# A hybrid attention, state-space and expert-retrieval block on one core: three groups of token tiles instead of four, and a reordered start

## The chip, the cores and the metric

The kernel runs on one core of one Trainium2 chip. The metric is the device time of one execution in microseconds (us). The engines are called TensorE (PE; PEld its weight loads), VectorE (DVE), ScalarE (ACT), GpSimd (POOL) and SyncE (SP). SP issues most transfers, POOL the gathers.

## What is computed

One block over 1024 latent tokens and 256 context tokens, 1024 wide, all in float32:

```python
z_lat = modulate(h_lat, sh_a, sc_a) @ w_in      # query, kv, rope key, state-space input, two gates
z_ctx = modulate(h_ctx, csh_a, csc_a) @ w_in
att_lat = block_attention(q_l, concat([k_c, k_l]), concat([v_c, v_l]))   # 8 heads, 1280 keys
s5_lat, s5_ctx = s5_mixer(su_l, su_c, ...)      # both directions, complex diagonal, 32 groups
out_lat = branch_merge(att_lat, s5_lat, gm_l, gs_l, w_glu, w_out)
h_lat = layer_norm(ALPHA * h_lat + g_a * out_lat, ln1_g, ln1_b)
f_lat = peer(modulate(h_lat, sh_f, sc_f), wq, keys, u_tab, v_tab)
h_lat = layer_norm(ALPHA * h_lat + g_f * f_lat, ln2_g, ln2_b)
```

`peer` finds for each token and each of 8 heads the 16 best of 16384 experts by product keys, 128 experts a token, takes the dot product of the token with each expert's row of `u_tab`, and sums the experts' rows of `v_tab` with the gelu of these products as weights.

## The kernel before, in words

The latent tokens lie in eight tiles of 128, the context in two. The program is one function, `block_kernel`. Each engine works its instructions off in a fixed order, which the compiler's scheduler makes from the order of the code, from priorities (`tc.high_priority(PRIO[gi])`, one offset a group) and from `tc.issue_after(...)`, which lets what stands under it come only behind a given instruction.

**The start (L118 to L330).** Large weights go through `wload` (L214), 1 MB tiles of a pool `w` with four buffers. `load_x` (L246) loads two token tiles with one such transfer, so they take weight buffers too. Eight 1 MB tiles of the modulation weights `w_mod_a` (L278) are multiplied with the condition into the bank `pmr` (L282). Four ACT copies (L292) bring its four rows to `mrow`, four transposes (L295) make `pm`, and VectorE turns it into the column `modc` (L297, L300). For each of ten tiles, `project` (L302) then normalises (L175), transposes, writes the modulated tile `hm` (L318, L320), stores it to `hm_d`, and multiplies it with the state-space part of the input weights (`pc`, L327), whose result goes to `us_d`. Beside this, `modulation_rows` (L349) works through 16 further 1 MB weights.

**The state space (L364 to L660).** VectorE and POOL build tables of powers (L367 to L491). The input is reloaded as `U` by eight transfers of 16 x 32 x 192 (L651). `compress` (L660) reloads `hm` tile by tile (L664) and makes compressed keys and values; the state products (L582, L583) need `U` and the tables.

**Groups (L1404).** `front` takes a group of token tiles through attention (scores L858 to L862, their maxima L863, probabilities L805, weighted values L809), the gates (products L239 to L241), and `close` (output product L954), and hands back a generator, `route`: the expert query (`pqr` L1066, `pz` L1074) and the two top-16 searches (L994 to L998). That generator is stepped `TSTEP` times at each step of the next group's attention. Each group loads all keys, values, gate and output weights, and splits keys and weights anew into two parts (L233 on ACT, L234 on VectorE). `PREP` says how early the next group's query projection (`prepare`, `pa` L770) begins.

**Retrieval.** For tiles 0 and 1, POOL gathers for each of 128 expert numbers one row per token from `peer_u` (L1271, tile `ub`), VectorE multiplies and sums (L1275, a "score"), and then POOL gathers rows of `peer_v` token by token (L1351), which TensorE sums (`acc` L1356, a "weighted row"). `HOLDS` keeps scores behind marks in the routes. Tiles 2 to 5 take another way: their weights are spread into a table (`spread`, L1147 to L1156), and `dense` goes over all experts (`turn` L1235 to L1237, `fd` L1196 to L1198) with the retrieval of tiles 6 and 7 on VectorE beside it.

The order is set by tables at the head of the file:

```python
GROUPS = ((0,), (1, 2), (3, 4, 5), (6, 7))
TSTEP = (2, 2, 2)
SUBS = (((0,),), ((0, 1),), ((0, 1, 2),), ((0, 1),))
PRIO = (0, 1500, 1500, 3000, 2000)
HOLDS = {0: [(M0, S0)] + [("r1.%d" % h, S0 + P0 * (h + 1)) for h in range(8)], ...}
```

Of the kernel before, what the change touches and what calls it, by code (L numbers as in the profile page):

```python
# [8 lines left out]
F32 = mybir.dt.float32  # L9
# [21 lines left out]
WBUFS = 4  # L31
# [3 lines left out]
SCB = (3, 3, 2, 2)  # L35
SC2 = (1, 1, 1, 1)
CAB = (1, 1, 1, 1)
OHB = (1, 1, 1, 1)
QHB = (2, 2, 1, 1)
H2B = 1  # L40
HMB = 2
GROUPS = ((0,), (1, 2), (3, 4, 5), (6, 7))
DENSE = (2, 3, 4, 5)
VEC = (6, 7)
TSTEP = (2, 2, 2)
TPRE = (0, 0, 0)
# [27 lines left out]
S0 = 36
P0 = 128
S1 = 100
P1 = 128
M0 = "p2"
M1 = "p3"
# [3 lines left out]
KENG = ((), (), (), ())  # L83
GENG = ((), (), (), ())
# [5 lines left out]
def block_kernel(ctx: ExitStack, tc: tile.TileContext, a: dict, out: bass.AP):  # L90
# [163 lines left out]
    SY.dma_start(bcol, a["b_col"])  # L254
# [13 lines left out]

    load_x(0)
# [5 lines left out]
    GP.memset(mrow, 0.0)  # L275
    pmr = bank("mm", "pmr")
    for k in range(8):
        wt = wload(a["w_mod_a"][k], [128, 2048])  # L278
        if k == XLOAD:
            load_x(1)  # L280
        for j in range(4):
            PE.matmul(pmr[32 * j:32 * j + 2, :], sil[:, k, :], wt[:, j * 512:(j + 1) * 512],  # L282
                      start=(k == 0), stop=(k == 7), tile_position=(0, 32 * j))
    with tc.issue_after(last[0].ins if hasattr(last[0], 'ins') else last[0]):
        w1 = s5.tile([128, 8, 512], F32, tag="U", name="w1")
        for k in range(0, 8, 2):
            SY.dma_start(w1[:, k:k + 2, :], a["w_in1"][:, k:k + 2, 384:896])
# [12 lines left out]
    V.tensor_scalar(modc[:, 1], modc[:, 1], 1.0, None, op0=ADD)  # L300

    def project(n):  # L302
        lat = n - 2
        ctxt = lat < 0
        cond = 1 if ctxt else 0
        if n % 2 == 0:
            if n > 2:
                load_x(n // 2)
            normalize(xt[n:n + 2])
# [12 lines left out]
        transpose8(x, put, "S")  # L322
        S.dma_start(hm_d[n], hm.rearrange("p a b -> p (a b)"))
# [43 lines left out]
    V.tensor_scalar(cni, cni, -1.0, None, op0=MUL)  # L367
# [123 lines left out]
    V.tensor_tensor(dsk, dsk, eye[0:16, 0:16].unsqueeze(1).to_broadcast([16, 32, 16]), op=MUL)  # L491

# [154 lines left out]
    wk = [wload(a["w_ukv"][:, k, :], [128, 2048]) for k in range(2)]  # L647
    U = s5.tile([128, 32, 192], F32, tag="U", name="U")
# [114 lines left out]
    def prepare(gi, P, w, hms):  # L763

        cqT = R["q"][1]
        for i, hmT in enumerate(hms):
# [4 lines left out]
            nq = (P or W).tile([128, 384 if P else 2048], F32, tag="nq" if P else "w", bufs=2 if P else WBUFS, name="nq")[:, 0:384]  # L771
# [9 lines left out]
        if P:  # L781
            P.release()
# [812 lines left out]
```

## Time and profile before

| | |
|---|---|
| runs | 3733.66, 3748.12, 3753.72 us, median 3748.12 |
| profiled execution | 3734.93 us, span of the trace 3733.2 us |
| instructions | 54383 |
| mean granted TensorE clock | 0.948 |
| busy share | TensorE 90%, VectorE 79%, GpSimd 40%, ScalarE 35% |
| moved | 1032.46 MB, 277 GB/s over the span |
| of it gathers | 536.94 MB in 1024 gathers |

The stages follow one another on TensorE: start and projections to about 180 us, state space, keys and values to 473, group (0) to 645, group (1, 2) to 981, attention of (3, 4, 5) to 1341, its gates to 1520 and close to 1628, attention of (6, 7) to 1924, its gates to 2064, the spread to 2212, and the dense part to the end. A stage's rows say more than the shares of the whole run.

### The profile page before, as it was taken

Reading aid. Unit: us, or ns where it says so; the run is one execution under the profiler, and the core shown is the slowest. Engines: PE = TensorE matmul, PEld = TensorE weight load, DVE = VectorE, ACT = ScalarE, POOL = GpSimd, SP = SyncE. Lnnn points to the kernel's source line nnn. Section 1 sums busy time; section 2 is a strip of 40 time slices with the busy share of each in tenths; the row PEclk is TensorE's granted clock in tenths of the full one; section 3 lists DMA queues with packets and bytes.
Section 4 is the critical chain, followed back from the end, with each engine's and each line's share of the span. In section 5 each row is a group of like instructions: output and inputs, shape, how many; then the busy total and the mean of one; then the engine's idle time right before and its main releaser. Section 6 shows DMA issues by size and latency. Waiting matters only on the chain.

```text
span 3733.2 us, 54383 instructions
## 1 busy us (share of the span) xinstructions
PE 3359.1 (90%) x20022; PEld 2733.2 (73%) x20022; DVE 2956.9 (79%) x6996; ACT 1297.7 (35%) x2329; POOL 1491.9 (40%) x1254
## 2 busy tenths in 40 slices
PE   5978888979779989869999969999999999999997
PEld 3745577869667668757769758878888888888885
DVE  7358755685798879689968877888888888889895
ACT  2223353443123444033345443333333333333332
POOL 5045400041355564443442100265655555546540
PEclk7978999989889989979999979999999999999998
DMA  8742276476698898987898763599999999989992
GB/s 280 236 85 73 89 264 228 156 301 244 224 347 309 316 338 324 362 308 289 295 355 314 296 232 124 181 368 340 330 342 333 339 335 340 340 325 355 340 328 79
DMA packets 348714, 1032.46 MB, mean 277 GB/s; under 512 B 46592, under 2 KB 142080, under 8 KB 322592
## 3 DMA queue, kind: packets, MB, share of 16 engines
q0 software_dynamic: 147456, 536.94, 39.3%
q1 hardware_dynamic: 164032, 462.20, 34.9%
q10 hardware_dynamic: 36960, 29.86, 2.5%
q8 instruction: 157, 2.57, 0.3%
q14 instruction: 109, 0.89, 0.1%
HBM read 961.27 MB, written 67.62 MB: 276 GB/s over the span
## 4 chain that ended last, share of the span: by engine, by line
PE 56%; DVE 9%; issue 8%; DMA 7%; ACT 2%; POOL 2%; DVEq 0%; POOLq 0%; ACTq 0%
PE turn L1235 6%; PE turn L1237 6%; PE turn L1236 6%; PE fd L1196 5%; PE fd L1197 5%; PE fd L1198 5%; DMA vb<-in_peer_v,eiT 4%; DVE ub L1275 3%; PE po L954 2%; PE acc L1356 2%; PE pqr L1066 2%; PE pe L1153 2%; DMA ub<-in_peer_u,ei 2%; POOL ub L1271 1%; PE po L809 1%
## 5 line engine op out<-in xcount | busy, mean ns | idle before, releaser
L1271 POOL DMA_INDIRECT ub<-in_peer_u,ei x512 | 654.9, 1279 | 1212.9 <-DVE ub L1275 438.4
L1275 DVE SCALAR_TENSOR_TENSOR ub<-ub,h 128x1024 f32<-128x1024 f32 x512 | 616.3, 1217 | 59.5 <-DMA ub<-in_peer_u,ei 59.2
L1318 POOL DMA_INDIRECT vb<-in_peer_v,ei x256 | 361.8, 1413 | 268.2 <-DVE f L1321 205.5
L1351 POOL DMA_INDIRECT vb<-in_peer_v,eiT x256 | 288.7, 1128 | 400.4 <-PE acc L1356 324.8
L1235 PE MATMUL turn<-hh,u 128*128 128x512 f32 x1024 | 401.7, 392 | 0.0
L1236 PE MATMUL turn<-hh,u 128*128 128x512 f32 x1024 | 400.2, 391 | 0.0
L1237 PE MATMUL turn<-hl,u 128*128 128x512 f32 x1024 | 400.1, 391 | 0.0
L1197 PE MATMUL fd<-v,kpe_l 128*128 128x512 f32 x887 | 351.7, 397 | 1.5 <-DVE kpe_l L234 1.5
L1198 PE MATMUL fd<-v,kpe_h 128*128 128x512 f32 x887 | 349.6, 394 | 0.0
L1196 PE MATMUL fd<-v,kpe_h 128*128 128x512 f32 x887 | 339.3, 396 | 0.0
L1321 DVE SCALAR_TENSOR_TENSOR f<-vb,zz,f 128x1024 f32<-128x1024 f32 x254 | 325.4, 1281 | 2.8 <-DMA vb<-in_peer_v,ei 0.2
L1239 ACT ACTIVATE act<-turn 128x512 f32<-128x512 f32 x128 | 76.6, 598 | 578.7 <-PE turn L1237 578.6
L233 ACT CAST v<-w 128x1024 fp32r<-128x1024 f32 x128 | 134.7, 1053 | 269.1 <-PE fd L1197 269.0
L1235 PEld LDWEIGHTS turn<-hh,u 128*128 128x128 f32 x1024 | 192.3, 188 | 42.0
L1237 PEld LDWEIGHTS turn<-hl,u 128*128 128x128 f32 x1024 | 192.3, 188 | 41.9
L1236 PEld LDWEIGHTS turn<-hh,u 128*128 128x128 f32 x1024 | 192.3, 188 | 40.4
L1356 PE MATMUL acc<-vb,diag 128*32 128x256 f32 x2048 | 159.8, 397 | 51.1 <-DMA vb<-in_peer_v,eiT 51.0
L1198 PEld LDWEIGHTS fd<-v,kpe_h 128*128 128x128 f32 x887 | 166.8, 188 | 41.4
L1196 PEld LDWEIGHTS fd<-v,kpe_h 128*128 128x128 f32 x887 | 166.9, 188 | 40.8
L1197 PEld LDWEIGHTS fd<-v,kpe_l 128*128 128x128 f32 x887 | 166.9, 188 | 40.5 <-DVE kpe_l L234 1.8
L234 DVE TENSOR_TENSOR v<-w,v 128x1024 fp32r<-128x1024 f32 x128 | 156.2, 1221 | 33.4 <-ACT v L233 32.8
L1241 DVE TENSOR_TENSOR act<-act,gt 128x512 f32<-128x512 f32 x128 | 88.6, 692 | 118.2 <-ACT act L1239 117.9
(421 smaller groups left out, 8143.2 us busy)
## 6 DMA issues: line engine op xcount, KB each, us to landing
w<-in_peer_uT SPq DMA_DIRECT2D x64, 1024.0 KB
w<-in_peer_v SPq DMA_DIRECT2D x64, 1024.0 KB
w<-in_peer_wq SPq DMA_DIRECT2D x32, 1024.0 KB
gT_d<-stage SPq DMA_DIRECT2D x16, 2048.0 KB
gt<-gT_d SPq DMA_DIRECT2D x32, 1024.0 KB
vh<-v_d SPq DMA_DIRECT2D x32, 640.0 KB
w<-k_d SPq DMA_DIRECT2D x32, 640.0 KB
w<-in_w_mod_b SPq DMA_DIRECT2D x16, 1024.0 KB
```

The lines of the kernel that those rows point to most:

```text
L1196: PE.matmul(o, ah[:, ts], vh[:, cs], start=first, stop=False)
L1197: PE.matmul(o, al[:, ts], vh[:, cs], start=False, stop=False)
L1198: return PE.matmul(o, ah[:, ts], vl[:, cs], start=False, stop=final)
L1235: PE.matmul(turn, uh[:, k, :], hh[:, k, :], start=(k == 0), stop=False)
L1236: PE.matmul(turn, ul[:, k, :], hh[:, k, :], start=False, stop=False)
L1237: PE.matmul(turn, uh[:, k, :], hl[:, k, :], start=False, stop=(k == 7))
L1271: GP.indirect_dma_start(out=ub, out_offset=None, in_=a["peer_u"], in_offset=bass.IndirectOffsetOnAxis(ap=ei[:, s:s + 1], axis=0))
L1275: V.scalar_tensor_tensor(ub, ub, 1.0, h2, op0=MUL, op1=MUL, accum_out=dots[:, s:s + 1])
L1318: GP.indirect_dma_start(out=vb, out_offset=None, in_=a["peer_v"], in_offset=bass.IndirectOffsetOnAxis(ap=ei[:, s:s + 1], axis=0))
L1321: V.scalar_tensor_tensor(f, vb, z[:, s:s + 1], f, op0=MUL, op1=ADD)
L1351: GP.indirect_dma_start(out=vb, out_offset=None, in_=a["peer_v"], in_offset=bass.IndirectOffsetOnAxis(ap=eiT[:, t:t + 1], axis=0))
L1356: PE.matmul(acc[d // 2][o:o + 32, 256 * (d % 2):256 * (d % 2) + 256], dg[:, q, jj, :], vb[:, d * 256:(d + 1) * 256], start=False, stop=Fal ...
```

## The change

The tiles are now taken in three groups, (0, 1, 2), (3, 4, 5) and (6, 7); the route of the first group runs in two parts, tile 0 and then tiles 1 and 2. The holds on the scores of tiles 0 and 1 are gone, the steps of the route per attention step are 3 and 2. At the start, token tiles are loaded into buffers that are still empty (`ckvT` and a widened `U`) with two 512 KB transfers a pair, the second pair and several small tables behind the last modulation weight, and the row `mrow` comes over in two copies of 128 x 256, one on ACT and one on VectorE. The second half of the state-space tables is issued only after `modc`. The first two reloads of `hm` stand ahead of `U`, further ones two tiles ahead of their use, and `U` comes in 32 pieces.

```diff
-GROUPS = ((0,), (1, 2), (3, 4, 5), (6, 7))
+GROUPS = ((0, 1, 2), (3, 4, 5), (6, 7))
-TSTEP = (2, 2, 2)
+TSTEP = (3, 2)
-SPLIT = (False, False, True, False)
-SUBS = (((0,),), ((0, 1),), ((0, 1, 2),), ((0, 1),))
+SPLIT = (False, True, False)
+SUBS = (((0,), (1, 2)), ((0, 1, 2),), ((0, 1),))
-PREP = (0, 9, 9, None)
+PREP = (9, 9, None)
-PRIO = (0, 1500, 1500, 3000, 2000)
+PRIO = (0, 1500, 3000, 2000)
-RAT = 3
+RAT = 2
-HOLDS = {0: [(M0, S0)] + [("r1.%d" % h, S0 + P0 * (h + 1)) for h in range(8)],
-         1: [(M1, S1)] + [("r2.%d" % h, S1 + P1 * (h + 1)) for h in range(8)],
-         6: [("t3", 0)]}
+HOLDS = {6: [("t2", 0)]}
...
-        x = wload((a["x"][2 * i - 2:2 * i] if i else a["ctx"]).rearrange("l p d -> p l d"), [128, 2, D])
-        xt.extend([x[:, 0, :], x[:, 1, :]])
+        pair = [w1x[:, 8 + 2 * j:10 + 2 * j].rearrange("p a b -> p (a b)") if i % 2 else ckvT[:, j] for j in range(2)]
+        for j, t in enumerate(pair):
+            SY.dma_start(t[:, 0:D], a["x"][2 * i - 2 + j] if i else a["ctx"][j])
+            xt.append(t[:, 0:D])
...
-    for j in range(4):
-        S.copy(mrow[32 * j:32 * j + 2, :], pmr[32 * j:32 * j + 2, :])
+    S.copy(mrow[:, 0:256], pmr[:, 0:256])
+    V.tensor_copy(mrow[:, 256:512], pmr[:, 256:512])
...
-    V.tensor_scalar(modc[:, 1], modc[:, 1], 1.0, None, op0=ADD)
+    held = V.tensor_scalar(modc[:, 1], modc[:, 1], 1.0, None, op0=ADD)
...
+    hold = tc.issue_after(held.ins)
+    hold.__enter__()
+    V.tensor_scalar(cni, cni, -1.0, None, op0=MUL)
...
+    hold.__exit__(None, None, None)
...
+    load_hm(0)
+    load_hm(1)
     U = s5.tile([128, 32, 192], F32, tag="U", name="U")
-    ul = us_d.rearrange("b (g c) l j -> l c (b g) j", c=16)
-    for l in range(8):
-        SY.dma_start(U[16 * l:16 * l + 16], ul[l])
+    for b in range(4):
+        ul = us_d[b].rearrange("(g c) l j -> l c g j", c=16)
+        for l in range(8):
+            SY.dma_start(U[16 * l:16 * l + 16, 8 * b:8 * b + 8], ul[l])
```

How the orders change, at three places. First SyncE's transfers at the end of the projections, before:

```order
L357 DMA mod_d<-rows 1x512 x4
L214 DMA w<-in_w_ukv 128x2048
L664 DMA hm<-hm_d 128x1024
L651 DMA U<-us_d 16x32x192 x7
L664 DMA hm<-hm_d 128x1024
L651 DMA U<-us_d 16x32x192
L664 DMA hm<-hm_d 128x1024 x4
```

and now:

```order
L354 DMA mod_d<-rows 1x512 x4
L652 DMA hm<-hm_d 128x1024 x2
L660 DMA U<-us_d 16x8x192 x32
L533 DMA T<-kd_d_74 128x8x64
L652 DMA hm<-hm_d 128x1024 x3
```

The second `hm` has moved from behind seven pieces of `U` to ahead of all; the third stands behind all 32.

Second, VectorE around the column `modc` (lines 404 to 490 before are tables), before:

```order
L409 TENSOR_TENSOR pwi<-sq_1243,sq_1244 128x32
L297 TENSOR_TENSOR modc<-pm,bcol 128x32
L462 TENSOR_TENSOR sq_1243<-aim 128x32
L489 COPY ri<-pwi 64x256
L490 COPY ri<-pwi 64x256
L300 TENSOR_SCALAR modc<-modc 128x16
L463 TENSOR_TENSOR kf<-kf,sq_1243 128x32
L320 TENSOR_SCALAR hm<-tp,modc 128x128 x3
```

and now:

```order
L429 COPY uli<-u8i 128x32
L287 COPY mrow<-pmr 128x256
L292 TENSOR_TENSOR modc<-pm,bcol 128x32
L295 TENSOR_SCALAR modc<-modc 128x16
L452 MEMSET pwr 128x32
L453 MEMSET pwi 128x32
L454 TENSOR_TENSOR pwr<-mag,ucs 128x32
L315 TENSOR_SCALAR hm<-tp,modc 128x128 x3
```

`modc` was VectorE's instruction 222 and is now its 151st; the powers `pwr`, `pwi` and all behind them have moved past it.

Third, VectorE at the first score (the instruction that reads `ub`; `mx` are attention's maxima, `ef` and `ei` the end of a route), before, where it stands after 55 of 192 maxima:

```order
L799 TENSOR_REDUCE smx_6414<-sm3_6329 128x1
L863 TENSOR_REDUCE mx_6384<-pS_6385 128x1
L800 RECIPROCAL smx_6414<-smx_6414 128x1
L1275 SCALAR_TENSOR_TENSOR ub_17881,dots_17878<-ub_17881,h2_17879 128x1024
L863 TENSOR_REDUCE mx_6384<-pS_6392 128x1
L863 TENSOR_REDUCE mx_6384<-pS_6399 128x1
```

and now, after 108 of 192:

```order
L1045 SCALAR_TENSOR_TENSOR ef_7341<-pi_8301 128x64
L1114 CAST ei_8538<-ef_7341 128x128
L1120 CAST eiT_8542<-ptE_8540 128x128
L1286 SCALAR_TENSOR_TENSOR ub_17492,dots_17489<-ub_17492,h2_17490 128x1024
L1005 MAX V16_8553<-sc_8578 128x8 x2
L1286 SCALAR_TENSOR_TENSOR ub_17495,dots_17489<-ub_17495,h2_17490 128x1024
```

The first score has moved from the attention of tiles 1 and 2 into the middle of that of tiles 3 to 5, between the route of tile 0 and those of tiles 1 and 2. Counted over VectorE's whole order, 167 scores stood ahead of the 145th maximum (the end of that attention) and 131 do now, all of them behind the 108th.

## Rows read from the trace of the kernel before

**Rows 1.** Busy time by stretch of the run; x is the count of instructions.

```profile
core 0: us, PE busy (x) PEld busy (x) DVE busy (x) ACT busy (x) POOL busy (x), PEclk, DMA share, GB/s
60.00:210.00 150.00, 120.91 (x939) 96.85 (x938) 55.26 (x146) 31.39 (x67) 28.32 (x37) 0.89 0.82 229
180.00:218.00 38.00, 15.54 (x46) 9.12 (x46) 2.35 (x13) 3.12 (x10) 0.00 (x0) 0.69 1.00 124
480.00:560.00 80.00, 67.21 (x429) 60.20 (x429) 46.79 (x123) 48.55 (x123) 0.00 (x0) 0.89 0.78 287
560.00:660.00 100.00, 83.14 (x568) 75.59 (x567) 56.91 (x121) 35.30 (x60) 0.00 (x0) 0.97 0.62 226
660.00:850.00 190.00, 161.31 (x1091) 145.24 (x1089) 146.70 (x495) 86.18 (x229) 52.83 (x40) 0.94 0.64 230
850.00:980.00 130.00, 117.45 (x838) 111.93 (x838) 74.03 (x173) 30.52 (x43) 1.87 (x2) 0.95 0.57 203
981.00:1341.00 360.00, 304.99 (x2178) 244.00 (x2176) 317.93 (x1045) 125.39 (x326) 204.91 (x183) 0.93 0.89 323
1341.00:1520.00 179.00, 156.99 (x1292) 142.58 (x1292) 147.59 (x308) 70.76 (x79) 89.39 (x65) 0.93 0.91 342
1520.00:1628.00 108.00, 77.62 (x458) 58.44 (x458) 85.83 (x229) 8.89 (x17) 53.12 (x44) 0.83 0.87 322
1628.00:1924.00 296.00, 281.44 (x2189) 214.26 (x2190) 239.55 (x1073) 116.30 (x281) 130.18 (x127) 0.98 0.85 307
2064.00:2212.00 148.00, 106.73 (x776) 88.21 (x766) 123.17 (x362) 66.54 (x81) 18.33 (x18) 0.86 0.71 264
```

**Rows 2.** Groups of TensorE, 20 to 60 us: busy, mean ns, idle before and releaser.

```profile
L295 PE MATMUL pm<-eye,mrow 128*128 128x128 f32 x4 | 1.1, 428 | 6.9 <-ACT mrow L292 6.9
L327 PE MATMUL pc<-hm,w 128*128 128x128 f32 x26 | 5.3, 384 | 6.6 <-DVE hm L320 6.6
```

**Rows 3.** Timeline, 38 to 60 us: start, length, engine, line, operation, idle before.

```profile
38.06 1.89 PE L282 MATMUL pmr<-w,sil 128*2 128x512 f32 x8 [1.86 <-DMA w<-in_w_mod_a]
41.73 2.37 ACT L175 ACTIVATE w<-w,off,rs_y 128x1024 f32<-128x1024 f32 x2 [19.26 <-DMA w<-in_w_in]
44.39 2.34 ACT L292 COPY mrow<-pmr 2x512 f32<-2x512 f32 x4
```

**Rows 4.** TensorE's group after the projections, then tile U: ns min/median/max, first and last start.

```profile
L668 PE MATMUL pb<-w,hm 128*128 128x320 f32 (+1 forms) x56 | 19.6, 508 | 18.5 <-DMA hm<-hm_d 18.5
L651 SPq DMA_DIRECT2D U<-us_d x8: 334/654/3927, 180.5 to 193.6; - x8
L582 PE MATMUL pS<-U,Pm x32: 299/299/351, 217.9 to 232.6; 128*64 128x160 f32 x32
```

**Rows 5.** Timeline: the first product of tile 0's query projection.

```profile
472.87 2.36 PE L770 MATMUL pa<-w 128*128 128x128 f32 x19 [0.72 <-ACT zt L639]
```

**Rows 6.** Groups of TensorE and VectorE, 981 to 1341 us.

```profile
L1066 PE MATMUL pqr<-h2T,w 128*128 128x128 f32 x512 | 62.7, 277 | 1.9 <-ACT att L810 1.4 <-ACT qh L1070 0.5
L1074 PE MATMUL pz<-keysT,qh 128*128 128x128 f32 x64 | 10.5, 286 | 2.0 <-ACT sc L1075 1.4 <-ACT att L810 0.5
L1356 PE MATMUL acc<-vb,diag 128*32 128x256 f32 x416 | 30.6, 387 | 5.1 <-DMA vb<-in_peer_v,eiT 5.0
L1275 DVE SCALAR_TENSOR_TENSOR ub<-ub,h 128x1024 f32<-128x1024 f32 x133 | 160.7, 1216 | 16.2 <-DMA ub<-in_peer_u,ei 16.1
L863 DVE TENSOR_REDUCE mx<-pS 128x1 f32<-128x512 f32 (+1 forms) x72 | 41.7, 593 | 5.7 <-PE pS L862 5.7
```

**Rows 7.** All score gathers by their line, and the page's row of their queue.

```profile
L1271 POOL DMA_INDIRECT ub<-in_peer_u,ei x512: 932/1144/2957, 766.6 to 3224.7; - x171
q0 software_dynamic: 147456, 536.94, 39.3%
```

**Rows 8.** Transfers: the gather queue 473 to 980 us, then all from 980 to 2212 us.

```profile
q0 software_dynamic: 6048, 22.02, 11.8%
...
DMA packets 97118, 389.44 MB, mean 316 GB/s; under 512 B 10304, under 2 KB 16704, under 8 KB 88896
```

More of the change, by code (lines that the diff above doesn't have):

```diff
@@ L34 @@
 RB = 6
[L35 to L39, printed above, removed]
+SCB = (2, 2, 2)
+SC2 = (1, 1, 1)
+CAB = (1, 1, 1)
+OHB = (1, 1, 1)
+QHB = (1, 1, 1)
 H2B = 1
 HMB = 2
-GROUPS = ((0,), (1, 2), (3, 4, 5), (6, 7))
+GROUPS = ((0, 1, 2), (3, 4, 5), (6, 7))
 DENSE = (2, 3, 4, 5)
 VEC = (6, 7)
-TSTEP = (2, 2, 2)
-TPRE = (0, 0, 0)
+TSTEP = (3, 2)
+TPRE = (0, 0)
 CHUNK = 32
@@ L50 @@
 VCUT = 2
-STB = (1, 1, 1, 1)
-SPLIT = (False, False, True, False)
-SUBS = (((0,),), ((0, 1),), ((0, 1, 2),), ((0, 1),))
+STB = (1, 1, 1)
+SPLIT = (False, True, False)
+SUBS = (((0,), (1, 2)), ((0, 1, 2),), ((0, 1),))
 CENG = "VVVV"
@@ L61 @@
 XLOAD = 4
-GSIDE = ('right', 'right', 'right', None)
-CSIDE = ("right", "right", "right", None)
+GSIDE = ('right', 'right', None)
+CSIDE = ("right", "right", None)
 SETTLE = 2
-PREP = (0, 9, 9, None)
-GSPLIT = (True, True, True, True)
+PREP = (9, 9, None)
+GSPLIT = (True, True, True)
 GWB = 2
-EBS = (2, 2, 2, 4)
+EBS = (2, 2, 4)
 EBANK = "S"
-PRIO = (0, 1500, 1500, 3000, 2000)
+PRIO = (0, 1500, 3000, 2000)
 PACE = 8
-RAT = 3
+RAT = 2
 TWAIT = 2
[L74 to L79, printed above, removed]
-HOLDS = {0: [(M0, S0)] + [("r1.%d" % h, S0 + P0 * (h + 1)) for h in range(8)],
-         1: [(M1, S1)] + [("r2.%d" % h, S1 + P1 * (h + 1)) for h in range(8)],
-         6: [("t3", 0)]}
-KENG = ((), (), (), ())
-GENG = ((), (), (), ())
+HOLDS = {6: [("t2", 0)]}
+KENG = ((), (), ())
+GENG = ((), (), ())
 EVERY = (1, 2, 1)
@@ L253, in block_kernel @@
     bcol = pre.tile([128, 16], F32, tag="bcol", name="bcol")
-    SY.dma_start(bcol, a["b_col"])
     S.activation(sil, ccT, func=AF.Tanh, scale=0.5)
@@ L267, in block_kernel @@
     dsk = s5.tile([16, 32, 16], F32, tag="dsk", name="dsk")
+    w1x = s5.tile([128, 12, 512], F32, tag="U", name="w1")
     load_x(0)
@@ L284, in block_kernel @@
     with tc.issue_after(last[0].ins if hasattr(last[0], 'ins') else last[0]):
-        w1 = s5.tile([128, 8, 512], F32, tag="U", name="w1")
+        w1 = w1x[:, 0:8]
+        SY.dma_start(bcol, a["b_col"])
         for k in range(0, 8, 2):
-            SY.dma_start(w1[:, k:k + 2, :], a["w_in1"][:, k:k + 2, 384:896])
+            loaded = SY.dma_start(w1[:, k:k + 2, :], a["w_in1"][:, k:k + 2, 384:896])
+    with tc.issue_after(loaded.ins):
+        load_x(1)
+        SY.dma_start(iota, a["iota"])
+        V.tensor_copy(ranks, iota[:, 0:16].unsqueeze(2).to_broadcast([128, 16, 16]))
         for t, nm in ((bre, "s5_b_re"), (bim, "s5_b_im"), (cre, "s5_c_re"), (cni, "s5_c_im")):
@@ L305, in project @@
         cond = 1 if ctxt else 0
[L306 to L309, printed above, removed]
+        if n == 0:
+            normalize(xt[0:2])
+        if n % 2 and n + 2 < NT:
+            normalize(xt[n + 1:n + 3])
         x = xt[n]
@@ L322, in project @@
         transpose8(x, put, "S")
+        if n % 2 and n // 2 + 2 < NT // 2:
+            load_x(n // 2 + 2)
         S.dma_start(hm_d[n], hm.rearrange("p a b -> p (a b)"))
@@ L647, in block_kernel, with load_hm @@
     wk = [wload(a["w_ukv"][:, k, :], [128, 2048]) for k in range(2)]
+    hms = []
+    def load_hm(n):
+        hms.append(pre.tile([128, 8, 128], F32, tag="hm", bufs=HMB, name="hm"))
+        SY.dma_start(hms[n].rearrange("p a b -> p (a b)"), hm_d[n])
+    load_hm(0)
+    load_hm(1)
     U = s5.tile([128, 32, 192], F32, tag="U", name="U")
-    ul = us_d.rearrange("b (g c) l j -> l c (b g) j", c=16)
-    for l in range(8):
-        SY.dma_start(U[16 * l:16 * l + 16], ul[l])
-    SY.dma_start(qng, a["q_norm_g"])
+    for b in range(4):
+        ul = us_d[b].rearrange("(g c) l j -> l c g j", c=16)
+        for l in range(8):
+            SY.dma_start(U[16 * l:16 * l + 16, 8 * b:8 * b + 8], ul[l])
     kng = pre.tile([128, 2], F32, tag="kng", name="kng")
-    SY.dma_start(kng, a["kv_norm_g"])
     ropt = pre.tile([128, 8, 128], F32, tag="ropt", name="ropt")
-    SY.dma_start(ropt, a["rope_tok"])
+    with tc.issue_after(loaded.ins):
+        SY.dma_start(qng, a["q_norm_g"])
+        SY.dma_start(kng, a["kv_norm_g"])
+        SY.dma_start(ropt, a["rope_tok"])
     def compress(n):
@@ L662, in compress @@
         ctxt = lat < 0
-        hm = pre.tile([128, 8, 128], F32, tag="hm", bufs=HMB, name="hm")
-        SY.dma_start(hm.rearrange("p a b -> p (a b)"), hm_d[n])
+        hm = hms[n]
         pb = bank("mm", "pb")
@@ L668, in compress @@
             PE.matmul(pb[:, 0:w], hm[:, k, :], w1b[k // 4][:, k % 4, 0:w], start=(k == 0), stop=(k == 7))
+        if n + 2 < NT:
+            load_hm(n + 2)
         junk = pre.tile([128, 256], F32, tag="junk", name="junk")
@@ L748, in prepare_loads @@
         grp = GROUPS[gi]
-        P = pool("P%d" % gi) if gi else None
+        P = pool("P%d" % gi)
         SY.dma_start(R["q"][2], a["rope_feat"][:, :, 128 * grp[0]:128 * grp[0] + 128 * len(grp)])
@@ L753, in prepare_loads @@
             w = [w[:, 0], w[:, 1], wload(a["w_cq"][2], [128, 8, 128])]
-            return P, w, [wload(hm_d[grp[0] + 2].rearrange("p (a b) -> p a b", a=8), [128, 8, 128])]
+            two = wload(hm_d[2:4].rearrange("l p (a b) -> p l a b", a=8), [128, 2, 8, 128])
+            return P, w, [two[:, 0], two[:, 1], wload(hm_d[4].rearrange("p (a b) -> p a b", a=8), [128, 8, 128])]
         w = P.tile([128, 3, 8, 128], F32, tag="wcq", name="wcq")
@@ L770, in prepare @@
                     PE.matmul(pa[:, j * 128:(j + 1) * 128], hmT[:, k, :], w[j][:, k, :], start=(k == 0), stop=(k == 7))
-            nq = (P or W).tile([128, 384 if P else 2048], F32, tag="nq" if P else "w", bufs=2 if P else WBUFS, name="nq")[:, 0:384]
+            nq = P.tile([128, 384], F32, tag="nq", bufs=2, name="nq")
             ss = cols.tile([128, 1], F32, tag="ss", name="ss")
@@ L780, in prepare @@
                 S.activation(cqT[:, j, i * 128:(i + 1) * 128], pt[:, j, :], func=AF.Copy, scale=qng[:, j:j + 1])
-        if P:
-            P.release()
+        P.release()
     def open_queries(gi):
```

7 lines of the change are left out of this document (1 added, 6 removed).

## The prediction

> **What bounds the kernel now.** I read the busy time of each engine in stretches first, since one average over 3733 us hides different limits. From 180 to 218 us almost nothing runs: TensorE 15.5 of 38 us, VectorE 2.4, while the transfer engines are 1.00 busy for only 124 GB/s. From 480 to 980 us, attention, gates and output projection of tile 0 and then of tiles 1 and 2, no engine is full: TensorE is busy 67.2 of 80, 83.1 of 100, 161.3 of 190 and 117.5 of 130 us, and the transfer share is 0.57 to 0.78. From 981 to 1341 us, attention of tiles 3 to 5 with the routes of tiles 1 and 2 and the score gathers of tiles 0 and 1 beside it, VectorE (317.9 of 360) and the transfers (0.89, 323 GB/s) are both near full; after that TensorE or the transfers are [rows 1]. The dense part after 2212 us keeps its instructions, and its inputs come from a finished table, so I cost the change there at nothing.
>
> The second view is who ended each idle time. At the start TensorE waits 6.9 us for ACT's copy of the modulation row and 6.6 us for VectorE's first `hm` [rows 2]; ACT had been held 19.3 us by a load that its normalisation needed, and its four copies take 2.3 us [rows 3]. Behind the projections TensorE waits 18.5 us for the reload of `hm`, the second of which SP issues behind seven of the eight `U` transfers [rows 4].
>
> **The change part by part.** The sum is made against the profiled execution, 3734.9 us (span 3733.2); the median of the runs shown is 3748.1, 13 us above it. A difference of about 0.5%, 19 us, is what a measurement of this kernel can tell from no change.
>
> *Start.* The second token pair now stands behind most modulation weights, so the last weight may land a little sooner, which I leave out. ACT is no longer in the middle of its normalisation when the row is ready: the last product ends at 39.95 and the first copy starts at 44.39, 4.4 us, and the copies take 2.3 [rows 3]. Two half copies, one on each of two engines, cost some 0.5 us (an estimate from 0.58 us for one of the four). That gives 4.4 + 1.8. VectorE reaches `modc` and `hm` without the second half of the tables in front of them: 6.6 us [rows 2]. Together −13. Bounds: −15, and 0 if the stream of modulation weights behind it sets the pace to 210 us (share 0.82, 229 GB/s); TensorE's 120.9 of 150 us speaks for most of it staying [rows 1]. The held table work moves to where VectorE is busy 55.3 of 150 us [rows 1]: nothing, unless the state space comes to wait for it.
>
> *Into the state space.* Two `hm` reloads now stand ahead of `U`, and the first state product needs one quarter of `U`. Before, it starts at 217.9 us [rows 4]. Now TensorE has two tiles of compression and the products (0.3 us each) to do while `U` lands. But `hm` of the third tile is issued behind all 32 pieces, and one issue of `U` takes SP 0.65 us at the median [rows 4]: 21 us, so to about 202 with the projections' end at 181. I take −20 of the 22 us that TensorE idles there. Bounds: −24, and 0, since the transfer engines are full at 124 GB/s [rows 1] and may end `U` no sooner. If each piece costs its issue, 24 more pieces are 16 us, and the term becomes −4. The Trainium skill, "DMA: Bandwidth & Descriptors", section "Rules for kernel authors", speaks against this edit too: it asks for transfers of at least a MiB and calls those under 64 KB mostly overhead, and here pieces of 384 KB become 96 KB; no row shows `U` in such pieces, and by that rule the sum would lean to the −12 that a term of −4 gives.
>
> *Three tiles in one group.* The two groups ahead of tiles 3 to 5 take 508 us, from 473 [rows 5] to 981. TensorE is busy 429 us from 480 to 980 [rows 1]; the route of tile 0 moves out, half of the 73.2 us that two routes take later [rows 6], and 392 us stay. Keys, values, gate and output weights are loaded and split once instead of twice, which is off TensorE. Its busy share was 0.84 in attention with one tile, 0.90 in the gates of two, 0.95 beside routes (281.4 of 296) [rows 1]; three tiles in turn, without a route, I put at 0.94: 415 us, so −93. Bounds 0.98 and 0.86: 400 and 456, −108 and −52.
>
> *What is pushed into the next group.* Attention of tiles 3 to 5 now carries three routes instead of two. Its first half has tile 0's route and no score, as the order shows. TensorE's work of that half is (305.0 − 30.6 for `acc` − 73.2 for the two routes) / 2 + 36.6 for one route = 137 us [rows 1, 6], at 0.94 some 147. In the second half fall as many scores as this stage had before (131): 160.7 us of VectorE. Its other 157 us of 317.9 were attention and two routes; the maxima are 41.7 of it [rows 6], and I put attention at 75 (an estimate), half of it now past: 160.7 + 82 + 37 = 280, on an engine nearly full 290. The stage: 147 + 290 = 437 against 360, so +77. Bounds: 260 to 330 for the second half, +47 to +117.
>
> *Later stages.* In the new order 10 more scores fall beside the close of group 1, 27 more beside the attention of tiles 6 and 7, and some 20 more weighted rows into the last stretch. Ten times 1.216 us [rows 6] on a VectorE busy 85.8 of 108 [rows 1]: +10. Twenty-seven, 33 us, on one busy 239.6 of 296, where TensorE ends the stage [rows 1]: +9, bounds 0 and +35. A weighted row is eight products, 30.6 / 52 = 0.6 us of TensorE [rows 6], 20 are 12 us in a stretch with 106.7 of 148 busy [rows 1]: +2, bounds −5 and +12.
>
> Sum: −13 − 20 − 93 + 77 + 10 + 9 + 2 = −28. On the profiled execution that is 3707, on the median 3720; I say **3715**.
>
> **The rivals.**
> *Nothing is gained* (chance 0.22). Retrieval starts when the first tile's route is ready: at 767 us now [rows 7], about 473 − 33 + 415 + 147 = 1002 then. From 980 to 2212 us 389 MB moved, 316 GB/s; 42 gathers (22 MB) came earlier [rows 8]. In the new order these come later too, and half an attention's keys and values (5 MB) earlier: 406 MB stand behind the first gather. My forecast asks for 406 MB in 1182 us, 343 GB/s; at 336 dense begins at 2212 as before, and the head start of 235 us is given back: 3730 to 3760. For it: transfers 0.85 to 0.89 busy in every stage between. Against it: 1341 to 1520 ran at 342 with TensorE at 157.0 of 179 [rows 1], so transfers alone did not set the pace.
>
> *Slower* (0.18). The same queue, one step on: with the gathers packed closer, the transfers stay at the 323 of the stage from 981 to 1341 us, and 406 MB take 1257 us. Dense begins at 2259, +47: 3782 to 3795. It decides from about 330 GB/s down, as a mean from the first gather to the dense part.
>
> *Much more* (0.14). VectorE fills its gaps (42 us idle of 360 [rows 1]), the second half takes 260, the later stages absorb the extra rows, and three tiles run at 0.98: −13 − 20 − 108 + 47 + 10 = −84, or 3651 to 3664.
>
> *The start does not hold* (0.06). `U` in 32 pieces or the held tables delay the state space, the first two terms fall to −4 together, and the sum to +1: 3736 to 3749.
>
> **How the numbers follow.** The forecast (3690 to 3735) keeps 0.40. "Much more" and the bounds of the terms give the low end 3655; half of "slower" the high end 3782. Faster by over 19 us holds "much more" and nearly all of the forecast: 0.53. Slower by as much holds "slower" and the upper edge of "nothing": 0.19. Same: 0.28.
>
> **What would show it.** Right: the first product of the input projection at about 42 us instead of 54.6, the first state product before 190, attention of tiles 3 to 5 starting near 855 instead of 983 and lasting about 437; the first gather near 1002, and 340 GB/s from there to the dense part. Wrong: if nothing is gained by 473 us, one of the two first terms fell; if the stage of tiles 3 to 5 lasts over 480 us with VectorE waiting for `ub`, the transfers set it; if VectorE is busy there without a wait and the stage is as long, I undercounted its route work.

## The result: 0.7% slower, and the profile after

The changed kernel takes 3767.3 us (median of 7 runs, 3755.8 to 3784.5), the kernel before, in runs beside it, 3741.1 us: a ratio of 1.0069 (95% interval 1.0044 to 1.0094), 26 us slower where 33 us faster than the first median was forecast. The profiled execution has a span of 3754.0 us, 20.8 us above that of before.

This is the changed kernel by stretch, cut at its own stages; it answers to [rows 1]:

```profile
core 0: us, PE busy (x) PEld busy (x) DVE busy (x) ACT busy (x) POOL busy (x), PEclk, DMA share, GB/s
34.00:166.00 132.00, 113.08 (x892) 96.14 (x892) 80.86 (x224) 34.28 (x66) 39.28 (x52) 0.88 0.74 264
166.00:205.00 39.00, 36.87 (x231) 26.11 (x230) 22.37 (x52) 11.41 (x37) 6.72 (x11) 0.87 0.85 155
486.00:683.00 197.00, 176.87 (x1128) 151.63 (x1127) 87.03 (x222) 111.53 (x282) 0.00 (x0) 0.98 0.26 89
683.00:794.00 111.00, 108.22 (x900) 107.81 (x901) 43.37 (x64) 32.78 (x43) 0.00 (x0) 1.00 0.45 162
868.00:1015.00 147.00, 135.30 (x904) 116.89 (x905) 90.49 (x384) 61.31 (x177) 0.99 (x1) 0.97 0.36 123
1015.00:1147.00 132.00, 105.03 (x709) 92.02 (x707) 120.43 (x421) 35.86 (x95) 72.34 (x67) 0.91 0.89 321
1147.00:1240.00 93.00, 32.24 (x128) 25.73 (x127) 91.78 (x253) 4.17 (x12) 71.42 (x56) 0.61 0.93 334
1240.00:1335.00 95.00, 73.54 (x591) 49.58 (x591) 70.17 (x263) 27.75 (x74) 55.44 (x54) 0.89 0.86 314
1335.00:1494.00 159.00, 146.79 (x1211) 132.96 (x1210) 142.04 (x295) 69.61 (x76) 81.78 (x57) 0.95 0.93 356
1605.00:1936.00 331.00, 296.21 (x2161) 219.74 (x2157) 279.35 (x1144) 119.96 (x285) 174.58 (x158) 0.92 0.89 320
```

Read it from the top. The hole of 38 us behind the projections is gone (36.9 of 39 us busy). Attention and gates of three tiles run with TensorE busy 177 of 197 and 108 of 111 us, and from the first query projection at 452 up to 1015 us POOL does nothing and the transfers are busy for less than half of the time (0.26 to 0.45 in these rows). Then the opposite: from 1015 to 1240 us VectorE is busy 212 of 225 us, the transfers 0.89 and 0.93, POOL issues gathers again, and between 1147 and 1240 us TensorE works 32 of 93 us. Who held it is in TensorE's timeline of that stretch (start, length, operation, idle before and its releaser):

```profile
1143.15 3.74 PE L1077 MATMUL pqr<-h2T,w 128*128 128x128 f32 x32
1146.72 0.38 PE L816 MATMUL pt<-eye,P 128*128 128x128 f32 x2
1172.48 1.22 PE L1085 MATMUL pz<-keysT,qh 128*128 128x128 f32 x4 [25.38 <-ACT sc L1086]
1174.22 6.43 PE L1077 MATMUL pqr<-h2T,w 128*128 128x128 f32 x32 [0.52 <-ACT qh L1081]
1183.63 1.22 PE L1085 MATMUL pz<-keysT,qh 128*128 128x128 f32 x4 [2.98 <-ACT sc L1086]
1185.37 6.00 PE L1077 MATMUL pqr<-h2T,w 128*128 128x128 f32 x32 [0.52 <-ACT qh L1081]
1200.75 1.22 PE L1085 MATMUL pz<-keysT,qh 128*128 128x128 f32 x4 [9.39 <-ACT sc L1086]
1202.49 5.97 PE L1077 MATMUL pqr<-h2T,w 128*128 128x128 f32 x32 [0.52 <-ACT qh L1081]
1223.01 1.23 PE L1085 MATMUL pz<-keysT,qh 128*128 128x128 f32 x4 [14.54 <-ACT sc L1086]
1224.75 4.21 PE L832 MATMUL pq<-cqT,w 128*128 128x384 f32 x6 [0.52 <-ACT qh L1081]
```

and in the waits of all engines from 1120 to 1250 us (total, times, longest):

```profile
ACT sc L1086 <- DVE sc L1007: 56.5, 5, 20.1
PEld pz L1085 <- ACT sc L1086: 53.1, 4, 25.6
PE pz L1085 <- ACT sc L1086: 52.3, 4, 25.4
ACT sc L1086 <- DVE I L1006: 24.3, 1, 24.3
```

VectorE's largest group from 1147 to 1240 us is the scores:

```profile
L1286 DVE SCALAR_TENSOR_TENSOR ub<-ub,h 128x1024 f32<-128x1024 f32 x56 | 67.6, 1213 | 2.3 <-DMA ub<-in_peer_u,ei 2.2
```

The chain reads backwards: TensorE's route product `pz` waits for ACT to empty its bank into `sc`; ACT waits for a free `sc`, which the top-16 search on VectorE (L1006, L1007) still reads; and VectorE, 91.8 of 93 us busy, spends 67.6 of them on 56 scores that stand in its order between the searches. Attention stands behind `pz` in TensorE's order: its next product, `pq`, comes at 1224.75 us.

Stage by stage, from the two profiled executions (attention runs from its first query product `pq` to its last product of weighted values; the close ends at the next first `pq`):

| stage | before | after | change | forecast |
|---|---|---|---|---|
| start to the first query projection | 473 | 452 | −21 | −33 |
| from there to attention of tiles 3 to 5 | 473 to 983 | 452 to 868 | −94 | −93 |
| attention of tiles 3 to 5 | 983 to 1341, 358 | 868 to 1335, 467 | +109 | +77 |
| its gates and close | 1341 to 1628, 287 | 1335 to 1609, 274 | −13 | +10 |
| attention of tiles 6 and 7 | 1628 to 1924, 296 | 1609 to 1936, 327 | +31 | +9 |
| to the first dense product | 294 | 293 | −1 | +2 |
| dense to the end | 1515 | 1525 | +10 | 0 |
| sum | | | +21 | −28 |

The transfers tell the same. From the first gather (1014 us) to the dense part:

```profile
L1282 POOL DMA_INDIRECT ub<-in_peer_u,ei x512: 932/1146/3477, 1014.0 to 3238.5; - x171
...
DMA packets 97884, 404.07 MB, mean 333 GB/s; under 512 B 10801, under 2 KB 13177, under 8 KB 89465
```

404 MB at 333 GB/s is 1214 us: a higher rate than before ([rows 8], 316), and still too low to win back the 247 us by which the first gather comes later [rows 7].

### The profile page after: what moved, and what is told of

Same layout as the page of the kernel before. It is cut to its first block, busy times and chain, and to the rows that moved or that the text cites. A ratio compares the mean times of both kernels' runs of the same rounds, so it can differ in the third digit from the quotient of the medians.

```text
span 3754.0 us, 53950 instructions
## 1 busy us (share of the span) xinstructions
PE 3383.2 (90%) x19926; PEld 2734.1 (73%) x19926; DVE 2923.0 (78%) x6930; ACT 1259.1 (34%) x2270; POOL 1480.3 (39%) x1253
## 4 chain that ended last, share of the span: by engine, by line
PE 69%; DVE 16%; DMA 7%; issue 3%; ACT 3%; POOL 1%; ACTq 0%; DVEq 0%; SPq 0%; POOLq 0%
PE turn L1246 6%; PE turn L1247 6%; PE turn L1248 6%; PE fd L1208 5%; PE fd L1207 5%; PE fd L1209 5%; DVE ub L1286 4%; DMA ub<-in_peer_u,ei 3%; PE po L820 2%; DMA vb<-in_peer_v,eiT 2%; PE pe L1164 2%; PE acc L1367 2%; PE pqr L1077 2%; PE po L965 2%; PE pq L832 2%
## 5 line engine op out<-in xcount | busy, mean ns | idle before, releaser
L1367 PE MATMUL acc<-vb,diag 128*32 128x256 f32 x2048 | 169.2, 412 | 40.1 <-DMA vb<-in_peer_v,eiT 39.3
L1207 PEld LDWEIGHTS fd<-v,kpe_h 128*128 128x128 f32 x887 | 167.0, 188 | 41.5 <-ACT kpe_h L223 0.5
```

Source lines behind the costliest of these rows:

```text
L1207: PE.matmul(o, ah[:, ts], vh[:, cs], start=first, stop=False)
L1367: PE.matmul(acc[d // 2][o:o + 32, 256 * (d % 2):256 * (d % 2) + 256], dg[:, q, jj, :], vb[:, d * 256:(d + 1) * 256], start=False, stop=Fal ...
```

## The experiments

The kernel before has medians between 3737 and 3762 us on the chips of these runs, 0.7% apart, so runs are compared by their ratio to the kernel before on the same chip; stages come from one profiled execution each.

**One half alone.** The first pair keeps one half of the change and puts the other back. `start_only` has the tables of before (`GROUPS`, `SUBS`, `TSTEP`, `PRIO`, `HOLDS`, the buffer counts and the rest that go by group) and its `prepare_loads` and `prepare`; `groups_only` has the code of before from the start to `compress` (`load_x`, `mrow`, the order of the tables, the reloads of `hm`, `U`).

> The four groups of the kernel before with the changed start alone (empty buffers, weights first, held tables, early hm, U in pieces). In the changed kernel the first query projection began at 452 us instead of 473. Theory A (the head start is kept, since TensorE and the chain of attention set the pace up to 980 us): the same 21 us sooner there, and 15 to 21 us faster at the end, about 3722. Theory B (gathers by the transfers or VectorE set the end, so a head start before them is lost): 3735 to 3747, no difference.

Measured: 0.9989 (0.9975 to 1.0003). Theory B: of the head start 9 us are left at most, and perhaps nothing.

> The three groups of the changed kernel with the start of the kernel before. Theory A: the start's 15 to 21 us are missing, 3783 to 3790, so the grouping alone costs some 45 us. Theory B: the end is set behind the first gather by queues that do not care when they begin, 3762 to 3772, as the changed kernel.

Measured: 1.0086 (1.0066 to 1.0105). The grouping is what costs, some 32 us, about as much as the whole change (1.0069); what the start gives it back is not told apart by these intervals. On the chip of the first result this ratio is 3773 us: 1 us outside theory B's range and 10 below theory A's.

**VectorE or the transfers.** The next two take half of one resource away from the scores of tiles 0 and 1.

```diff
-                V.scalar_tensor_tensor(ub, ub, 1.0, h2, op0=MUL, op1=MUL, accum_out=dots[:, s:s + 1])
+                hw = D // 2 if l < 2 else D
+                V.scalar_tensor_tensor(ub[:, 0:hw], ub[:, 0:hw], 1.0, h2[:, 0:hw], op0=MUL, op1=MUL, accum_out=dots[:, s:s + 1])
```

> The changed kernel with the scores of tiles 0 and 1 taken over 512 of the 1024 columns (half of each dot product is left out); all gathers stay. That is 256 times about 0.6 us, 150 us less on VectorE, and no byte less. Theory V (VectorE, full from 1015 to 1240 us, sets the stage of tiles 3 to 5): that stage 50 to 80 us shorter, the end 3670 to 3710. Theory T (transfers at 320 to 356 GB/s set it): the stage within 15 us, the end 3750 to 3770.

Measured: 1.0015 (1.0000 to 1.0029), 0.5% below the changed kernel. Half a hit: the stage is 80 us shorter (first attention product to last 881 to 1258, against 878 to 1335), as theory V has it, but by the ratio the end is 3747, not 3670 to 3710. In the stage's second half:

```profile
1015.00:1258.00 243.00, 188.51 (x1166) 162.51 (x1165) 204.21 (x904) 67.08 (x179) 128.31 (x130) 0.87 0.91 327
```

VectorE is down to 204 of 243 us, the transfers stay at 0.91 and 327 GB/s. But the end gains only some 20 us: the last weighted row of tiles 0 and 1 comes at 2308 us instead of 2208, inside the dense part. With cheaper scores the scheduler also wrote another order (85 instead of 128 scores ahead of the 132nd maximum), and order alone can move the end of attention, as `after_tstep2` below shows. But the first gate product comes 78 us sooner here (1276 instead of 1354) and 24 us sooner there. So VectorE paces this stage for the most part; that the transfers come next is read from their share and not shown by a run.

```diff
-            ub = rows.tile([128, D], F32, tag="row", name="ub")
-            GP.indirect_dma_start(out=ub, ...)
+            if l > 1 or s % 2 == 0:
+                ub = rows.tile([128, D], F32, tag="row", name="ub")
+                GP.indirect_dma_start(out=ub, ...)
```

> The changed kernel with every second score gather of tiles 0 and 1 left out (two scores use one gathered tile, so half the experts' products are missing); VectorE's work stays. That is 128 times 0.524 MB, 67 MB, some 200 us of transfer at 335 GB/s. Theory T: the stages behind the first gather 60 to 120 us shorter, the end 3650 to 3710. Theory V: within 20 us of the changed kernel, 3745 to 3770.

Measured: 1.0115 (1.0090 to 1.0140), slower than the changed kernel and outside both expectations. Inconclusive: with cheaper gathers the scheduler wrote another order, 78 scores ahead of the 114th maximum where there were 21, and attention of tiles 3 to 5 stretched from 457 to 500 us. It says nothing of the transfers, and fits with scores on VectorE holding up the attention that they are placed ahead of.

**The place of the scores and the buffers.** Three runs on the wait at 1147 us.

```diff
-TSTEP = (3, 2)
+TSTEP = (2, 2)
```

> The changed kernel with the routes of the first group stepped twice, not three times, at each attention step. By the order 41 scores instead of 128 then stand ahead of the 132nd maximum, and 67 instead of 129 ahead of the 144th. Theory Q (from 1147 to 1240 us the top-16 search stands behind scores on VectorE, the copy of sc waits for it, and attention waits behind the route's products in TensorE's queue): attention of tiles 3 to 5 gets 40 to 80 us shorter, and as the scores fall into later stages with gaps, the end is 15 to 35 us earlier than the changed kernel, a ratio to before of 0.997 to 1.003. Theory S (retrieval that starts late is simply moved, whatever its place): that stage shorter, the later ones longer by as much, ratio 1.005 to 1.009.

Measured: 1.0078 (1.0052 to 1.0104). Theory Q falls: attention does end early, at 1180 us, but the rest of the routes, with the scores between them, then runs without it, and the first gate product comes at 1330 us (1354 in the changed kernel). The ratio is theory S's. The hole only moved:

```profile
1015.00:1190.00 175.00, 140.53 (x992) 125.09 (x990) 163.69 (x525) 60.52 (x159) 104.43 (x88) 0.94 0.89 322
1190.00:1328.00 138.00, 65.07 (x461) 39.86 (x462) 128.73 (x442) 17.16 (x28) 95.12 (x80) 0.65 0.90 326
```

```diff
-HOLDS = {6: [("t2", 0)]}
+HOLDS = {0: [("r0.%d" % h, 8 * h + 8) for h in range(8)], 6: [("t2", 0)]}
```

> The changed kernel with the scores of tile 0 held behind the heads of the second route, eight a head: 72 instead of 128 ahead of the 132nd maximum, 128 as before ahead of the 144th. Theory Q: the wait of 1147 to 1240 us is spread out, attention of tiles 3 to 5 20 to 50 us shorter, ratio 1.000 to 1.005. Theory S: ratio 1.005 to 1.009.

Measured: 1.0234 (1.0204 to 1.0263), by far the worst, and outside both expectations. The 256th score comes at 1836 us instead of 1767: holding scores back made all of retrieval later.

```diff
-SCB = (2, 2, 2)
+SCB = (3, 2, 2)
-QHB = (1, 1, 1)
+QHB = (2, 1, 1)
```

> The changed kernel with the route's buffers of the first group as large as they were (three for sc, two for qh, instead of two and one). Theory Q with the buffers as cause: the 76 us that ACT waits for sc fall below 40 and the ratio to 1.000 to 1.004. If VectorE's order is the cause, the buffers only shift the wait by one step: ratio 1.005 to 1.009.

Measured: 1.0046 (1.0029 to 1.0063); ACT's wait for `sc` is still 58.0 us between 1015 and 1400. The ratio lies between the two expectations, and the intervals of this run and of the changed kernel overlap: the buffers may be worth 0.2%, but the wait stays without their shortage.

**Only the start of retrieval.** The kernel before, its early scores held back:

```diff
-S0 = 36
+S0 = 0
```

> The kernel before with all scores of tile 0 held until the query projection of tiles 3 to 5, so that the 26 to 36 scores that ran from 773 to 983 us fall behind it. Nothing else changes. Theory S (the late start of retrieval is what the grouping costs): 36 scores of 1.3 us on a VectorE that is 0.88 busy make it 25 to 50 us slower, ratio 1.006 to 1.013. If early scores are worth little, ratio 0.998 to 1.003.

Measured: 1.0079 (1.0050 to 1.0109), 29 us: theory S, in the lower half of its range. The first score moves from 773 to 965 us and nothing else is changed, and the time is that of the changed kernel within the intervals. The stretch from 640 to 840 us is left emptier (VectorE 122 us; 152 in a second profile of the kernel before, whose row stands last), the close of tiles 1 and 2 is as it was, and attention of tiles 3 to 5 is fuller and lasts some 30 us longer than before:

```profile
640.00:840.00 200.00, 178.23 (x1186) 159.82 (x1187) 122.05 (x455) 94.45 (x252) 5.80 (x6) 0.94 0.47 165
840.00:970.00 130.00, 117.19 (x825) 110.97 (x824) 73.52 (x175) 31.43 (x46) 2.86 (x2) 0.93 0.51 180
970.00:1357.00 387.00, 310.39 (x2134) 246.86 (x2133) 343.11 (x1088) 122.22 (x321) 230.68 (x203) 0.89 0.91 327
640.00:840.00 200.00, 170.57 (x1115) 152.12 (x1116) 152.37 (x510) 89.01 (x241) 46.14 (x36) 0.93 0.63 229
```

**No scores.** Both kernels without the scores of tiles 0 and 1:

```diff
+        if l < 2:
+            V.memset(dots, 0.5)
+            return
+            yield
```

> The kernel before without the 256 scores of tiles 0 and 1 (gathers and products left out, their results set to 0.5); the weighted rows stay. 311 us of VectorE and 134 MB less between 773 and 1689 us. Theory S: much faster, 3560 to 3640, and the yardstick for the next run.

> The changed kernel without the same 256 scores. Theory S (the grouping saves about 90 us up to the attention of tiles 3 to 5 and loses them to scores that start 245 us later): without scores to place, the saving stays, and this is 50 to 100 us faster than the kernel before without scores. Rival R (the third route and its buffers in the stage cost as much by themselves): within 20 us of it.

Measured: 0.9786 (0.9763 to 0.9809) and 0.9645 (0.9624 to 0.9666). The first is a miss: 3665 us where 3560 to 3640 were expected, so most of the scores' work was hidden in the kernel before. The second is theory S: without scores the changed kernel is 1.4% faster, 57 us between the medians. The same 256 scores with their gathers cost the kernel before 2.1% (some 80 us) and the changed one 4.2% (158 us); they take 311 us on VectorE. Gathers and products are left out together here, so this pair does not tell VectorE from the transfers. The stage of tiles 3 to 5 in the changed kernel without them:

```profile
868.00:1267.00 399.00, 384.12 (x3108) 288.32 (x3108) 236.28 (x1084) 136.81 (x369) 126.42 (x129) 1.00 0.70 249
```

TensorE is busy 384 of 399 us there at a granted clock of 1.00, with the third route in it. Rival R, that the route itself is the cost, is out.

**A version that beats both.** If a late start of retrieval costs, an earlier one should pay. The four groups, the new start, and more scores let through before the hold:

```diff
-S0 = 36
+S0 = 72
```

> The four groups with the changed start, and 72 instead of 36 scores of tile 0 let through ahead of the query projection of tiles 3 to 5 (by the order 85 instead of 49 scores ahead of the 73rd maximum). Theory S, turned round: scores moved forward into 850 to 980 us, where VectorE was busy 74 of 130, make it faster, ratio 0.988 to 0.996. If that stretch was already set by something else, 0.997 to 1.004.

Measured: 0.9946 (0.9926 to 0.9967), 3721.9 us beside 3743.1: 21 us faster than the kernel before. The close of tiles 1 and 2, here first and below it the kernel before in a second profile, shows where scores went (VectorE 112 instead of 79 of 140 us, the transfers 0.83 instead of 0.56):

```profile
840.00:980.00 140.00, 119.02 (x824) 110.91 (x823) 112.11 (x249) 31.70 (x46) 51.92 (x40) 0.91 0.83 316
```

```profile
840.00:980.00 140.00, 124.34 (x890) 118.25 (x889) 78.92 (x182) 34.94 (x51) 8.70 (x8) 0.94 0.56 202
```

> The same with all 128 scores of tile 0 let through (114 ahead of the 73rd maximum). Theory S with room left in that stretch: as start_s72 or better, 0.985 to 0.995; if VectorE fills up there and holds up the close of tiles 1 and 2, worse than start_s72, 0.995 to 1.005.

Measured: 1.0007 (0.9992 to 1.0022). The second expectation: too many, and the gain is gone. Attention of tiles 3 to 5 starts at 1019 us here and at 979 in `start_s72`.

> The kernel before, with 72 instead of 36 scores let through ahead of the query projection of tiles 3 to 5, and the old start. Theory S-place (the place of the early scores is worth the whole gain of start_s72, and the new start nothing): ratio 0.993 to 0.997. Theory S-room (the new start's 21 us are what makes room for the early scores, and 36 more without it only push): ratio 0.998 to 1.003.

Measured: 0.9984 (0.9967 to 1.0001), in the range of theory S-room. Neither edit is clear of no change alone (the start 0.1%, the hold 0.2%), both together are (0.5%). That they give more than their sum is not shown: the intervals of `before_s72` and `start_s72` touch. And the close of tiles 1 and 2 is as full here as in `start_s72` (VectorE 113 of 140 us, the transfers 0.88), so to fill that stretch is not yet the gain.

**Where the start's gain goes.** Side by side on one chip:

> The kernel before, for its stages on the same chip as the next two. Ratio 1.000; gates of tiles 6 and 7, dense start and end within 10 us of the first profile's 1949, 2218 and 3733.

> The changed start with the four groups, beside the kernel before on one chip, to see in which stage the head start goes. Theory S: it is still there when attention of tiles 3 to 5 begins (10 to 21 us) and at the last score of tile 1 less than 8 us are left, since the hold on the scores (36 until the next query projection) is the same. Rival: it is gone before that attention begins.

Measured: 3753.2 and 3756.6 us, one run each. The stages of the kernel before lie 15 to 18 us behind those of its first profile, not within 10. The expectation for the start was wrong and its rival nearer: the head start is 20 us at the first input projection, 9 at the end of the projections (168 against 177), 5 at the first query projection (464 against 469), and 3 at the attention of tiles 3 to 5. But this pair is an extreme one. The first query projection comes at 451 to 464 us in the twelve profiles with the new start (464 is this one) and at 468 to 478 in the six with the old; the middle ones are 455 and 471. So usually some 15 of the 20 us are left there. In the first profiles of `start_only` and of the kernel before 14 are left at the attention of tiles 3 to 5 (969 against 983), and none at its end (1345 against 1341). Where the rest goes differs from pair to pair, up to the end of that attention. First the kernel before, then the new start:

```profile
177.00:220.00 43.00, 21.19 (x70) 12.69 (x69) 5.15 (x26) 5.52 (x18) 0.00 (x0) 0.72 0.90 122
220.00:300.00 80.00, 74.18 (x411) 49.38 (x409) 74.53 (x120) 30.46 (x81) 48.67 (x51) 0.87 0.23 68
300.00:400.00 100.00, 84.62 (x466) 53.96 (x465) 82.14 (x122) 32.37 (x84) 63.16 (x67) 0.86 0.20 61
```

```profile
177.00:220.00 43.00, 40.39 (x237) 27.58 (x236) 35.56 (x71) 16.87 (x46) 19.33 (x19) 0.92 0.66 125
220.00:300.00 80.00, 67.97 (x349) 44.28 (x349) 67.15 (x108) 26.10 (x70) 43.88 (x56) 0.77 0.21 61
300.00:400.00 100.00, 83.77 (x429) 54.97 (x428) 81.83 (x118) 32.53 (x82) 61.26 (x70) 0.82 0.19 58
```

The hole at 177 us is filled (40.4 of 43 us), 30 us of VectorE's work with it, but from 220 us on the engines are less busy than before, and the granted TensorE clock is 0.77 and 0.82 instead of 0.87 and 0.86. That holds for the other profiles too: from 220 to 300 us the clock is 0.76 to 0.83 in all twelve with the new start, and 0.83 to 0.89 in all six with the old. TensorE's 96 key products from 220 to 470 us take 46.8 instead of 41.5 us with 11.5 us of waiting for ACT's copies ahead of them:

```profile
L724 PE MATMUL pk<-ckvT,w 128*128 128x512 f32 (+1 forms) x96 | 46.8, 629 | 11.5 <-ACT vt L718 6.9 <-ACT kt L727 4.7
```

> The changed kernel on the same chip, so that its stages and its ratio stand beside those of the other two. Ratio 1.005 to 1.009, its attention of tiles 3 to 5 some 115 us ahead of the kernel before at its start and within 15 us at its end.

Measured: 1.0066 (1.0041 to 1.0091), its attention of tiles 3 to 5 from 882 to 1345 us against 991 to 1340: the result again, 109 us ahead at the start of that stage and 5 us behind at its end.

## Why the prediction was wrong, point by point

- *Start and state space, −33.* Measured −21. The first term held: ACT copies the row at 31.5 us instead of 44.4, the first projection starts at 34 instead of 54.6 (42 was forecast), and the projections end at 166.2 instead of 180.5 us, −14 where −13 was forecast. The step that failed is "I take −20 of the 22 us that TensorE idles there". The hole is filled, the first state product comes at 177 instead of 218 us, but from the projections' end to the query projection it is 286 us instead of 292, so −7 (first before, then after):

```profile
180.50:472.90 292.40, 236.18 (x1219) 150.82 (x1217) 206.12 (x342) 96.94 (x247) 131.40 (x143) 0.87 0.35 84
166.20:452.20 286.00, 248.39 (x1270) 159.07 (x1271) 206.82 (x347) 98.89 (x251) 125.24 (x143) 0.86 0.34 91
```

  The condition under which the held tables were costed at nothing, "unless the state space comes to wait for it", came true. Of the 96 products that TensorE makes from these tables during the projections before, 49 stay there and the others now follow behind, and there TensorE waits 9.2 us for a table, VectorE's `Ei` (two rows before, then two after, in the same two stretches):

```profile
L520 PE MATMUL pk<-cre,Er 64*128 64x16 f32 (+1 forms) x144 | 22.2, 239 | 1.2 <-DVE Er L508 1.2
L520 PE MATMUL pk<-cni,Ei 64*128 64x16 f32 (+1 forms) x144 | 21.9, 238 | 0.0
L520 PE MATMUL pk<-cni,Ei 64*128 64x16 f32 (+1 forms) x168 | 27.2, 249 | 9.3 <-DVE Ei L511 9.2
L520 PE MATMUL pk<-cre,Er 64*128 64x16 f32 (+1 forms) x168 | 26.7, 246 | 1.9 <-ACT ks L524 1.6 <-DVE Er L508 0.3
```

  All products of this line together keep TensorE busy 36.6 us behind the projections instead of 29.4. That is read from rows; no run holds the tables alone, and the granted clock is lower there too (0.80 instead of 0.89 from 220 to 300 us). The preparation of three tiles then takes most of what is left: the first attention product comes at 486 instead of 490 us. The 32 pieces take SP 21 us, as forecast, though one issue is 0.30 us at the median and not 0.65; TensorE has other products meanwhile and waits 2.1 us for the `hm` behind them. The Trainium skill's rule on transfers of a MiB ("DMA: Bandwidth & Descriptors", "Rules for kernel authors") did not decide here. No run changes the pieces alone.
- *Three tiles in one group, −93.* Right in the sum, −94, with errors that cancel. 392 us at 0.94 are 417, so the term should have read −91. By the rows TensorE works 381 us of these 416, at 0.92: less work than forecast, at a lower share.
- *The stage of tiles 3 to 5, +77.* This is the step that turned the sign. Its first half was right (147 us; 137 at 0.94 are 146). Its second half has the VectorE work that was forecast, 282 us against 280, but takes 320 us and not 290, which lies inside the bounds of 260 to 330: the step "on an engine nearly full 290" took for granted that one full engine keeps the others supplied. It does not at the ends (70.2 of 95 us from 1240 on): when VectorE was through with scores and searches, attention, which had stood behind them on TensorE, still had to run. That is +109. These 30 us and the 13 of −20 and −7 above are 43 of the 49 us between the sum and what the two profiles show.
- *Later stages, +21.* In sum +27, with other parts: −13 in the gates and close, +31 in attention of tiles 6 and 7, +10 in the dense part (1515 us in the first profile and 1515 to 1526 in all the others but that of `after_half_sum`, whatever the kernel, so its spread). In tiles 6 and 7's attention 51 scores (61.6 us of VectorE) stand now and 16 (19.5) stood before, 35 more where 27 were counted:

```profile
L1286 DVE SCALAR_TENSOR_TENSOR ub<-ub,h 128x1024 f32<-128x1024 f32 x51 | 61.6, 1212 | 4.6 <-DMA ub<-in_peer_u,ei 4.6
```

```profile
L1275 DVE SCALAR_TENSOR_TENSOR ub<-ub,h 128x1024 f32<-128x1024 f32 x16 | 19.5, 1217 | 8.1 <-DMA ub<-in_peer_u,ei 8.0
```

  The +9 held that TensorE ends this stage and hides them. TensorE was busy 281 of 296 us then and is busy 296 of 331 now, so it no longer does; no run shows what does. `before_late`, which delays little but such early scores, costs about as much (29 us).
- *The rivals.* The account by bytes was the better model: 406 MB were counted behind the first gather, 404 moved, 336 GB/s was given as the rate at which nothing is gained, and 333 was reached, for a dense part 11 us later. The "slower" case named that mechanism, but with a rate of 323 and 3782 us at the least; 3767 lies between the two rivals. So the place of the loss was among the rivals at 0.22 and 0.18, and the forecast had put the sum of stages above it, though the sum asked for 343 GB/s, more than any long stage had shown. Its engine was not the transfers alone: halving the scores' VectorE time shortened the stage by 80 us. A share of the transfers beside VectorE is neither shown nor ruled out, since the run that was to test it changed the order.

## What to carry to other kernels

Before work is moved in front of the point at which a long queue can start, ask when that queue will start then: here attention was packed 94 us tighter in a region whose gaps no longer had anything to hold, and 256 scores cost 158 us instead of 80. Count what must pass behind the new start on each engine and on the transfers, and compare the rate that the forecast needs with what the best long stage has shown; a sum of stages that needs a higher one is not yet a forecast. Then turn the finding round: with the new start, moving 36 more of the early scores forward into gaps that stay was worth 0.5%, and moving all of tile 0's nothing.

## What was not expected of the hardware

With TensorE busy 32 of 93 us from 1147 to 1240, the granted clock was 0.61 as a mean of its two levels, so the few route products left in that stretch ran slower as well: 32 of `pqr` take 6.0 to 6.4 us there and 3.7 just before it. Without scores the whole stage had 1.00. In the state space filling a hole of 20 us was followed by a lower granted clock (0.77 against 0.87), where TensorE was a little less busy (68.0 and 74.2 of 80 us). Whether the clock or the waits came first in the state space is open. Nor was it tried why the new start and the larger hold gain together what neither gains alone.
